# TensorE's queue kept in the order of emission, with a new entry into each attention stage

## The chip, the cores and the metric

The kernel runs on one core of a Trainium2 chip. The metric is the device time of one execution in microseconds (us). Each engine of the core, TensorE (PE), VectorE (DVE), ScalarE (ACT), GpSimd (POOL) and SyncE (SP, which issues most DMAs), works through a queue of its own in order; an instruction whose input is not ready stands in its queue, and with it all that is behind it.

## The reference

Two identical layers act on a sequence of 256 tokens with 1024 features, in float32. One layer is:

```
h    = rmsnorm(x) ; proj = h @ w_in                      # 1024 x 7704
out_a = dilated_mixer(rope(rmsnorm(qa)), rope(rmsnorm(ka)), va)     # 24 heads of 64, 3 dilations
k_cmp, v_cmp = gelu(blocks of 32 tokens + pos @ cmp_w1) @ cmp_w2    # compressed keys and values
out_b = g0 * attention(qb, k_cmp, v_cmp) + g1 * attention(qb, k_sel, v_sel) + g2 * window(qb, k_win, v_win)
x = x + (sigmoid(m0) * (out_a @ w_proj_a) + sigmoid(m1) * (out_b @ w_proj_b)) @ w_out
h = rmsnorm(x) ; g, u = split(h @ w_up)                  # 1024 x 5632
x = x + (silu(causal_conv3(g)) * u) @ w_down             # 2816 x 1024
```

## The kernel before

**The weight stream.** All weights of a layer lie packed in units of 128 x 2048 floats, in the order of use. Each unit is loaded by SP in two halves into `raw` (five buffers, `load_half`), and `halve` in `prepare` splits each half into hi (ScalarE, L238) and lo (VectorE, L239), so that a float32 product is three fast matmuls: hi·hi, lo·hi and hi·lo (L290 to L292 with 512 columns of weights, L373 and L957 to L959 with 256 columns of tokens, L993 and L994 in the last projections). The splits lie in the list `pend`. `next_unit` hands out the next unit, loads the one after it, and casts at once what is due.

**The order of emission.** A layer's attention stage emits its weight chunks one after the other: c10 and c11 (compressed, selected and window keys and values, gates), bq (queries of mixer b), chunks 0 to 8 (q, k and v of mixer a), four merge units for mixer b after the chunks 1, 2, 3 and 5 (`merge`), projection b, four merge units for mixer a, projection a, `out_proj`; then `ffn_up` and `ffn_down`. A chunk of 512 columns is two units, each used for both token tiles, 12 matmuls a tile. After every group of matmuls the code calls `tick`, which casts one half and advances each attention job by one step, and starts a waiting one if fewer than five are active:

```
    def tick(depth=5):
        if pend:
            pend.popleft()[1]()
        for g in list(chains):
            advance(chains, g)
        for g in list(active):
            advance(active, g)
```

A job is a Python generator that emits some instructions and gives way at each `yield`: `rope_run` (normalise and rotate a tile of q or k, then its `fin` transposes it), `job_cmp1` (lays the compressed mixer's tokens out), `job_cmp2` (hidden layer, gelu, compressed attention), `job_b` (one head pair and token tile of selected and window attention), `job_a` (the same for the dilated mixer). So the code's own order puts a job's small matmuls between the groups of 12 or 24 stream matmuls, and `yield` sets how many groups lie between a job's steps.

**The order of the queues.** The order of emission is not the order of the queues. The framework lists the instructions of every engine anew: with a cost model of its own it takes for each engine the instruction that it holds to be ready first, and among ready ones the one emitted first. Waits on other engines are semaphores put in afterwards. In TensorE's queue of this kernel a stream matmul can therefore stand ahead of a job's matmul that the code emits before it.

**The entry of an attention stage.** In layer 0 the `start` pool holds the input (`xo`, with tokens in the order of residues), which SP loads between the first weight halves. `feed` scales it by the norm's gain into hi and lo parts of `hT`, squares it and sums the squares over the eight feature tiles: for tiles 0 to 3 of the first input the squares are GpSimd's, and the sums are GpSimd's too, but for the last (`fin`, VectorE, L333). `rstd_col` (L344) sums over partitions by two matmuls and takes the root on GpSimd; `dg` (L351, VectorE) is a diagonal matrix with the result, and `rstd_row` spreads it along the tokens by a matmul. Meanwhile GpSimd makes the rope tables `tabs` and `tabc` from `gr`, SP's load at L387. In layer 1 and ahead of the feed-forward, `feed` is called as the tiles of x are finished. In `rope_b`, `fin` copies the rotated keys into `rd` (L482) and at once transposes them (L485); `job_cmp1` copies into `cdup` (L792) and at once transposes (L795), then ScalarE copies the result into T2 in eight copies.

**job_cmp2.** L841 transposes the hidden layer, ScalarE copies it (L845), VectorE and a tanh (L851) make the gelu and `hr` (L855), L864 multiplies by cmp_w2, a chain of normalisation and rope ends with a copy (L876), L879 transposes, L891 scores, a softmax ends at `es` (L910), L914 transposes that. Between the steps stand one or two `yield`. It starts when the last w1 unit is through, and is emitted in the same ticks as `job_a`, whose eight exponentials are at L664.

Of the kernel before, what the change touches and what calls it, by code (L numbers as in the profile page):

```python
# [11 lines left out]
F32 = mybir.dt.float32  # L12
# [7 lines left out]
P = 128  # L20
D = 1024
S = 256
# [142 lines left out]
def block_kernel(ctx, tc, x_in, xo_in, ws, g_norm, g_rope, pos, w2, conv, rope_c, ropec_c, mask_c, misc_c, out):  # L165
# [17 lines left out]
    G.memset(warm, 0.0)  # L183
    A.activation(warm, warm, AF.Square)
    gain = com.tile([P, 2 * DEPTH, 8], F32, name="gain")
    ones = com.tile([P, P], F32, name="ones")
    G.memset(ones, 1.0)
    ident = com.tile([P, P], F32, name="ident")
    make_identity(nc, ident)
    masks = com.tile([P, 1152], F32, name="masks")  # L190
    misc = com.tile([P, 96], F32, name="misc")
# [23 lines left out]
    def prepare(upto):  # L215
        while nxt[0] < len(units) and nxt[0] <= upto:
            i = nxt[0]
            u = units[i][1:]
            ffn = u[0] in ("up", "down")
            if ffn and ffn_pool[0] is None:  # L220
                return
            if u[0] == "w1":
                split[i] = [load_half(i, c0, UW // 2) for c0 in (0, UW // 2)]
                nxt[0] += 1
                continue
            w = _unit_width(u)
            pool, nb = (ffn_pool[0], 1) if ffn and ffn_turn(i) else (com, 2)
            hi = pool.tile([P, UW], F32R, name="hi", bufs=nb)
            lo = pool.tile([P, UW], F32R, name="lo", bufs=nb)
            for c0 in (0, w // 2):  # L230
                if (i, c0) in early:
                    raw = early.pop((i, c0))
                else:
                    raw = load_half(i, c0, w // 2)
                c = slice(c0, c0 + w // 2)
# [69 lines left out]
    def feed(u, m, gi, permute, src=None):  # L305
# [6 lines left out]
        else:  # L312
            for t in range(2):
                tok = slice(t * P, (t + 1) * P)
                v = by_residue(src[:, m:m + 1, tok], t)[:, 0]
                hi, lo = [u[:, i, m, tok].rearrange("p (r i) -> p r i", r=4) for i in range(2)]
                A.activation(hi, v, AF.Copy, scale=gc)
                V.scalar_tensor_tensor(lo, v, gc, hi.bitcast(F32), op0=ALU.mult, op1=ALU.subtract)
        if m == 0:
            sums["acc"] = com.tile([P, S], F32, name="acc2", bufs=1)  # L320
        sq = sums["acc"] if m == 0 else com.tile([P, S], F32, name="sq", bufs=2)
        if src is not x and m < 4:
            G.tensor_tensor(sq, xm, xm, op=ALU.mult)
        else:
            A.activation(sq, xm, AF.Square)
        if m == 0:
# [14 lines left out]
    def rstd_col():  # L341
# [8 lines left out]
        for t in range(2):  # L350
            V.tensor_scalar(dg[:, t * P:(t + 1) * P], ident, r[:, 1, t:t + 1], None, op0=ALU.mult)  # L351
        sums["dg"] = dg
# [22 lines left out]
    def attention_layer(l, pool, hT):  # L375
# [16 lines left out]
        nc.sync.dma_start(w2t, w2[l].rearrange("p (a b d) -> p a b d", a=2, b=2))  # L392
        for a in range(2):
            G.tensor_tensor(tabs[:, a], cossin[:, a, :, None, :].to_broadcast([P, 2, 5, 64]),
                            gr[:, a, None, 0:5, :].to_broadcast([P, 2, 5, 64]), op=ALU.mult)
        tabc = pool.tile([P, 2, 64], F32, name="tabc")
        G.tensor_tensor(tabc, ropec, gr[:, :, 5, :], op=ALU.mult)
# [4 lines left out]
        qS = pool.tile([P, 2, 4, S], F32R, name="qS")  # L402
        bigF = pool.tile([P, 2, 16, 2, 16], F32, name="F", tag="bigF", bufs=1)
# [17 lines left out]

        def rope_run(raw, kind, t, nh, ksc, fin):
            t1 = pool.tile([P, 8, 64], F32, name="t1", bufs=4)[:, :nh]
# [9 lines left out]
            if ksc is None:  # L433
# [5 lines left out]
                            op=ALU.mult)  # L439
            V.tensor_add(t1, t1, t2)  # L440
            yield
            yield
            fin(t1)

        def chunk_in(c, ncols, post_fn):
            ps = [acc(), acc()]
            for kh in range(2):
                hi, lo = next_unit(1 if c == "c10" and kh == 1 else 2)
                hi = hi[:, :4 * ncols].rearrange("p (k n) -> p k n", k=4)
                lo = lo[:, :4 * ncols].rearrange("p (k n) -> p k n", k=4)  # L450
                for t in range(2):
                    for k in range(4):
                        kk = kh * 4 + k
                        tok = slice(t * P, (t + 1) * P)
                        mm3(ps[t][:, :ncols], hT[:, 0, kk, tok], hT[:, 1, kk, tok], hi[:, k], lo[:, k],
                            kh == 0 and k == 0, kh == 1 and k == 3)
                    if kh == 1:
                        if c == "c10" and t == 0:
                            nrm["col"] = rstd_col()
                        post_fn(t, ps[t])  # L460
# [17 lines left out]

        def rope_b(b, t):
            def fin(r):  # L480
                rd = pool.tile([P, 2, 2, 64], F32, name="rd", tag="t2", bufs=1)
                V.tensor_copy(rd, r[:, 0:2, None, :].to_broadcast([P, 2, 2, 64]))  # L482
                ps = att()
# [5 lines left out]
                ready["b"] += 1  # L489
            start(rope_run(kraw[:, t, b].rearrange("p (h d) -> p h d", d=64), 3 + b, t, 2, None, fin))  # L490

# [295 lines left out]
        def job_cmp1():  # L787
            for kv in range(2):
                ps = att()
                dup = pool.tile([P, 2, 2, 2, 64], F32, name="cdup", tag="pT", bufs=5)  # L790
                for h in range(2):
                    V.tensor_copy(dup[:, h], craw[:, :, 2 * kv + h, None, :].to_broadcast([P, 2, 2, 64]))  # L792
                for h in range(2):
                    for t in range(2):
                        T.transpose(ps[:, (2 * h + t) * P:(2 * h + t + 1) * P],  # L795
                                    dup[:, h, t].rearrange("p a d -> p (a d)"), ident)
                T2 = pool.tile([P, 2, 264], F32, name="T2", tag="pt", bufs=4)
                for t in range(2):
                    src = ps.rearrange("p (h t r i) -> p h t r i", h=2, t=2, r=4)[:, :, t]
                    for u in range(2):  # L800
                        c0 = t * P + 1 - u
                        A.copy(by_residue(T2[64 * u:64 * u + 64, :, c0:c0 + P], t), src[64 * u:64 * u + 64])
                if kv == 0:
# [32 lines left out]
        def job_cmp2():  # L836
# [85 lines left out]
            for i in range(2):  # L922
# [98 lines left out]
    def ffn_up(l, pool, u, act):  # L1021
# [135 lines left out]
```

## Time and profile before

| | |
|---|---|
| median of three runs | 968.22 us (965.47 to 968.27) |
| the profiled execution | 964.59 us |
| its span, first to last instruction | 962.8 us |
| granted TensorE clock, mean | 1.00 |
| busy: PE, DVE, ACT, POOL | 936.6, 753.0, 580.2, 154.7 us |
| DMA | 165.95 MB, 172 GB/s on average |

The times of single instructions come from the profiled execution, whose own time is 1.8 us longer than its span. The clock column is the share of full speed that the throttle granted. A matmul's recorded duration covers its way through the pipeline; successive ones overlap, so the distance between their starts is what each costs.

### The profile page before, as it was taken

To read this page: it belongs to the slowest core of one execution; us is meant where nothing else is said; L and a number is where in the kernel's file an instruction comes from. 1 tells how busy PE (TensorE), PEld (TensorE's weight loads), DVE (VectorE), ACT (ScalarE), POOL (GpSimd) and SP (SyncE) were. 2 spreads that over 40 slices of the span, in tenths; PEclk is the share of its full clock that TensorE was granted. 3 is DMA by queue.
4 is the path that set the end of the run, shared out by engine and by line. 5 is a ranking of instruction groups with operands and counts; after the bars stand their busy time and mean duration, and the time that the engine had idled before them with its cause. 6 is when DMAs were issued, how large, how long until landed. Compare 5 with 4: busy or idle time off the path is not lost.

```text
span 962.8 us, 18575 instructions
## 1 busy us (share of the span) xinstructions
PE 936.6 (97%) x7122; PEld 848.9 (88%) x7122; DVE 753.0 (78%) x1595; ACT 580.2 (60%) x1186; POOL 154.7 (16%) x179
## 2 busy tenths in 40 slices
PE   6899999999999999999998999999999999999998
PEld 4778887878999999999986787877799999999998
DVE  6898866887679889986478987678876888998742
ACT  6778665666556555555456986466755555655431
POOL 6140211212002111110122301122200111111000
PEclk9999999999999999999999999999999999999999
DMA  7734446525456565666455344554354465666660
GB/s 242 255 132 155 150 157 207 189 88 174 148 162 213 180 210 187 189 196 204 147 168 174 112 151 135 196 196 140 121 180 153 161 217 175 205 197 203 196 209 19
DMA packets 48041, 165.95 MB, mean 172 GB/s; under 512 B 6096, under 2 KB 7632, under 8 KB 47824
## 3 DMA queue, kind: packets, MB, share of 16 engines
q1 hardware_dynamic: 46800, 163.71, 52.1%
q8 instruction: 56, 0.92, 0.4%
q10 hardware_dynamic: 1152, 1.05, 0.3%
q14 instruction: 33, 0.27, 0.1%
HBM read 163.69 MB, written 1.05 MB: 171 GB/s over the span
## 4 chain that ended last, share of the span: by engine, by line
PE 78%; DVE 10%; ACT 6%; issue 2%; POOL 1%; DMA 1%; SPq 0%; DVEq 0%; ACTq 0%; POOLq 0%
PE acc L373 25%; PE acc L290 5%; PE acc L292 5%; PE acc L291 5%; DVE lo L239 4%; PE acc L1082 4%; PE acc L1084 4%; PE acc L1083 4%; PE acc L957 3%; PE att L571 3%; PE acc L959 3%; PE acc L958 3%; PE att L576 2%; PE acc L993 2%; PE acc L994 2%
## 5 line engine op out<-in xcount | busy, mean ns | idle before, releaser
L239 DVE TENSOR_TENSOR lo<-raw,hi 128x1024 fp32r<-128x1024 f32 (+1 forms) x292 | 368.4, 1279 | 51.6 <-ACT hi L238 49.4
L238 ACT CAST hi<-raw 128x1024 fp32r<-128x1024 f32 (+1 forms) x292 | 294.0, 1037 | 150.9 <-PE acc L291 36.9
L373 PE MATMUL acc<-u,hi 128*128 128x256 f32 x1376 | 236.3, 277 | 0.0
L373 PEld LDWEIGHTS acc<-u,hi 128*128 128x128 f32 x1376 | 207.4, 188 | 0.1
L373 PE MATMUL acc<-u,lo 128*128 128x256 f32 x688 | 190.2, 276 | 0.0
L290 PE MATMUL acc<-hi,hT 128*128 128x512 f32 (+1 forms) x384 | 154.0, 401 | 8.7 <-ACT hi L238 8.7
L292 PE MATMUL acc<-lo,hT 128*128 128x512 f32 (+1 forms) x384 | 150.0, 391 | 5.2 <-DVE lo L239 5.1
L291 PE MATMUL acc<-hi,hT 128*128 128x512 f32 (+1 forms) x384 | 148.5, 387 | 0.0
L373 PEld LDWEIGHTS acc<-u,lo 128*128 128x128 f32 x688 | 129.1, 188 | 0.0
L1084 PE MATMUL acc<-act,lo 128*128 128x256 f32 x352 | 97.2, 276 | 0.0
L1082 PE MATMUL acc<-act,hi 128*128 128x256 f32 x352 | 97.2, 276 | 0.0
L1083 PE MATMUL acc<-act,hi 128*128 128x256 f32 x352 | 97.2, 276 | 0.0
L290 PEld LDWEIGHTS acc<-hi,hT 128*128 128x128 f32 x384 | 72.6, 189 | 25.9 <-ACT hi L238 11.1
L292 PEld LDWEIGHTS acc<-lo,hT 128*128 128x128 f32 x384 | 72.4, 189 | 23.6 <-DVE lo L239 9.2
L291 PEld LDWEIGHTS acc<-hi,hT 128*128 128x128 f32 x384 | 72.7, 189 | 12.6 <-issue 0.3
L957 PE MATMUL acc<-hT,hi 128*128 128x256 f32 x256 | 73.4, 287 | 0.0
L959 PE MATMUL acc<-hT,lo 128*128 128x256 f32 x256 | 71.8, 281 | 0.0
L958 PE MATMUL acc<-hT,hi 128*128 128x256 f32 x256 | 71.7, 280 | 0.0
L1084 PEld LDWEIGHTS acc<-act,lo 128*128 128x128 f32 x352 | 66.1, 188 | 0.0
L1082 PEld LDWEIGHTS acc<-act,hi 128*128 128x128 f32 x352 | 66.1, 188 | 0.0
L1083 PEld LDWEIGHTS acc<-act,hi 128*128 128x128 f32 x352 | 66.1, 188 | 0.0
L1054 POOL TENSOR_TENSOR z<-z,rb 128x512 f32<-128x512 f32 x22 | 30.5, 1386 | 203.1 <-DVE z L1053 203.1
(215 smaller groups left out, 1690.2 us busy)
## 6 DMA issues: line engine op xcount, KB each, us to landing
raw<-in_ws_dram SPq DMA_DIRECT2D x300, 512.0 KB, 4.6
raw<-in_ws_dram SPq DMA_DIRECT2D x8, 280.0 KB, 4.2
x<-in_x_dram SPq DMA_DIRECT2D x1, 1024.0 KB, 9.6
out_dram<-x ACTq DMA_DIRECT2D x8, 128.0 KB, 2.7
gr<-in_g_rope_dram SPq DMA_DIRECT2D x2, 384.0 KB, 4.4
masks<-in_mask_dram SPq DMA_DIRECT2D x1, 576.0 KB, 7.6
xo<-in_xo_dram SPq DMA_DIRECT2D x2, 256.0 KB, 4.5
xo<-in_xo_dram SPq DMA_DIRECT2D x1, 512.0 KB, 7.0
```

The lines of the kernel that those rows point to most:

```text
L238: A.copy(h, r)
L239: V.tensor_sub(l, r, h.bitcast(F32))
L290: T.matmul(o, a_hi, b_hi, start=first, stop=False)
L291: T.matmul(o, a_lo, b_hi, start=False, stop=False)
L292: T.matmul(o, a_hi, b_lo, start=False, stop=last)
L373: return [lambda a=a: T.matmul(a[0], a[1], a[2], start=a[3], stop=a[4]) for a in todo]
L957: T.matmul(o, hi[:, k, ms], hT[:, 0, k], start=k == 0, stop=False)
L958: T.matmul(o, hi[:, k, ms], hT[:, 1, k], start=False, stop=False)
L959: T.matmul(o, lo[:, k, ms], hT[:, 0, k], start=False, stop=k == 7)
L1082: T.matmul(ps, hi[:, c], act[:, 0, k], start=k == 0, stop=False)
L1083: T.matmul(ps, hi[:, c], act[:, 1, k], start=False, stop=False)
L1084: T.matmul(ps, lo[:, c], act[:, 0, k], start=False, stop=k == NFT - 1)
```

## The change

Seven things are changed.

1. TensorE's instructions keep the order in which the code emits them (`manual_schedule` for PE). The other engines' queues are ordered as before.
2. The start: 14 idle matmuls on `ones`; the input's first loads and `gain` are issued from ScalarE's queue and the table load for Square stands behind them; SP's first four loads are quarters of a unit, and the first unit is cast in quarters, each ahead of the `feed` of one tile.
3. The input's squares are ScalarE's, two tiles at a time, and their sums VectorE's. `dg` goes to ScalarE.
4. `qS` is allocated ahead of the tables, so that it and not `gr` comes to lie where `xo` was. The tables are made in three steps, the later ones by a side job.
5. c10 goes through its first unit by k instead of by token tile, and calls rstd_col and both `post_c10` at its end; c11 goes by token tile.
6. `rd` is copied two ticks ahead of its transposes, `cdup` one tick; `job_cmp1` starts behind c11 instead of ahead of it, transposes with a permutation, and copies T2 in two copies a head pair instead of four. `job_b` waits one more tick.
7. Ahead of the feed-forward, rstd_col goes from place 42 of the first unit's 48 matmuls to place 3 of the second unit's; the row sum and the first gate move by three places.

```diff
@@ block_kernel
-    A.activation(warm, warm, AF.Square)
+    idle = att()
+    for i in range(14):
+        T.matmul(idle[:, 0:P], ones, ones, start=True, stop=True)
@@ prepare
-            for c0 in (0, w // 2):
+            step = w // 4 if (i, w // 4) in early else w // 2
+            for c0 in range(0, w, step):
@@ feed
+        if src is not x:
+            if m % 2:
+                sq = com.tile([P, 2, S], F32, name="sq2", bufs=2)
+                A.activation(sq, src[:, m - 1:m + 1], AF.Square)
+                if m > 1:
+                    V.tensor_add(sq, sq, sums["acc"])
+                sums["acc"] = sq
+            if m == 7:
+                sums["fin"] = com.tile([P, S], F32, name="fin", bufs=1)
+                V.tensor_add(sums["fin"], sq[:, 0], sq[:, 1])
+            return
...
-        if src is not x and m < 4:
-            G.tensor_tensor(sq, xm, xm, op=ALU.mult)
-        else:
-            A.activation(sq, xm, AF.Square)
+        A.activation(sq, xm, AF.Square)
@@ rstd_col
-            V.tensor_scalar(dg[:, t * P:(t + 1) * P], ident, r[:, 1, t:t + 1], None, op0=ALU.mult)
+            A.activation(dg[:, t * P:(t + 1) * P], ident, AF.Copy, scale=r[:, 1, t:t + 1])
@@ attention_layer
+            for t in range(2):
+                V.tensor_copy(by_residue(perm[:, t:t + 1], t)[:, 0], ident.rearrange("p (r i) -> p r i", r=4))
...
+        qS = pool.tile([P, 2, 4, S], F32R, name="qS")
         tabs = pool.tile([P, 2, 2, 5, 64], F32, name="tabs")
...
+        table(3, 5)
@@ rope_run
             V.tensor_add(t1, t1, t2)
+            if pre:
+                pre(t1)
             yield
             yield
             fin(t1)
@@ chunk_in
+            if c == "c11":
+                unit(0)
+                for t in range(2):
+                    for kh in range(2):
+                        if t == 0 and kh == 1:
+                            unit(1)
+                        mms(kh, t, range(4), kh == 0, kh == 1)
+                        if kh == 1:
+                            post_fn(t, ps[t])
+                        tick()
+                return
...
+                if c == "c10" and kh == 0:
+                    for k in range(4):
+                        for t in range(2):
+                            mms(0, t, [k], k == 0, False)
+                        if k % 2:
+                            tick()
+                    continue
@@ rope_b
+            def pre(r):
+                box["rd"] = pool.tile([P, 2, 2, 64], F32, name="rd", bufs=2)
+                V.tensor_copy(box["rd"], r[:, 0:2, None, :].to_broadcast([P, 2, 2, 64]))
@@ job_b
             while ready["b"] < 6:
                 yield
+            yield
@@ job_cmp1
-                ps = att()
                 dup = pool.tile([P, 2, 2, 2, 64], F32, name="cdup", tag="pT", bufs=5)
                 for h in range(2):
                     V.tensor_copy(dup[:, h], craw[:, :, 2 * kv + h, None, :].to_broadcast([P, 2, 2, 64]))
+                yield
+                ps = att()
...
-                                    dup[:, h, t].rearrange("p a d -> p (a d)"), ident)
+                                    dup[:, h, t].rearrange("p a d -> p (a d)"), perm[:, t])
...
+                for u in range(2):
+                    r = slice(64 * u, 64 * u + 64)
+                    A.copy(T2[r, :, 1 - u:1 - u + S], ps[r].rearrange("p (h q) -> p h q", h=2))
@@ attention_layer, its sequence
+        def job_tables():
+            table(2, 3)
+            yield
+            table(0, 2)
+            yield
+            G.tensor_tensor(tabc, ropec, gr[:, :, 5, :], op=ALU.mult)
...
         chunk_in("c10", 512, post_c10)
+        side.append(job_tables())
+        chunk_in("c11", 280, post_c11)
         side.append(job_cmp1())
-        chunk_in("c11", 280, post_c11)
@@ ffn_up
-                pg = unit({42: rstd_col}, True)
-                pu = unit({24: lambda: box.update(rb=rstd_row()), 30: lambda: post_g(0, pg)})
+                pg = unit({}, True)
+                pu = unit({3: rstd_col, 27: lambda: box.update(rb=rstd_row()), 33: lambda: post_g(0, pg)})
@@ block_kernel, its start
-        nc.sync.dma_start(xo[:, 0:2], xv[:, 0:2])
-        nc.sync.dma_start(gain, g_norm.rearrange("p (a k) -> p a k", k=8))
-        early[0, 0] = load_half(0, 0, UW // 2)
+        A.dma_start(xo[:, 0:2], xv[:, 0:2])
+        A.dma_start(gain, g_norm.rearrange("p (a k) -> p a k", k=8))
+        A.dma_start(xo[:, 2:4], xv[:, 2:4])
+        A.activation(warm, warm, AF.Square)
+        quarters(0, 0)
...
-        nc.sync.dma_start(xo[:, 2:4], xv[:, 2:4])
-        early[0, UW // 2] = load_half(0, UW // 2, UW // 2)
+        quarters(0, 1)
         nc.sync.dma_start(xo[:, 4:8], xv[:, 4:8])
...
+        prepare(0)
         for m in range(8):
-            if m in (1, 3):
-                if m == 1:
-                    prepare(0)
+            feed(hT, m, 0, False, xo)
+            if m < 4:
                 pend.popleft()[1]()
-            feed(hT, m, 0, False, xo)
@@ kernel
     with tile.TileContext(nc) as tc:
-        block_kernel(tc, *args)
+        with tc.manual_schedule(engines={mybir.EngineType.PE}):
+            block_kernel(tc, *args)
```

`quarters(i, h)` loads half h of unit i into one `raw` buffer by two DMAs of 512 columns each; `table(k0, k1)` makes the tables k0 to k1 - 1 with two multiplications on GpSimd.

## Rows read from the trace of the kernel before

**Rows 1.** The page's first part: busy time, share and instructions of each engine.

```profile
PE 936.6 (97%) x7122; PEld 848.9 (88%) x7122; DVE 753.0 (78%) x1595; ACT 580.2 (60%) x1186; POOL 154.7 (16%) x179
```

**Rows 2.** Busy time by stretch: PE, PEld, DVE, ACT, POOL, clock, DMA, GB/s.

```profile
40.00:60.00 20.00, 19.22 (x92) 15.25 (x91) 19.60 (x35) 12.87 (x21) 4.62 (x2) 1.00 0.63 210
...
340.00:360.00 20.00, 20.00 (x179) 20.00 (x178) 18.69 (x23) 10.78 (x16) 2.62 (x2) 1.00 0.62 199
```

**Rows 3.** TensorE's waits by releaser: total us, times, longest us.

```profile
PE acc L290 <- ACT hi L238: 8.7, 4, 7.1
PE acc L292 <- DVE lo L239: 5.1, 8, 2.2
PE att L344 <- DVE fin L333: 3.1, 2, 1.6
PE att L485 <- DVE rd L482: 2.6, 2, 1.8
PE att L795 <- DVE cdup L792: 1.9, 2, 1.5
```

**Rows 4.** Instructions in order of time, layer 0's entry: start, duration, engine, line.

```profile
7.08 0.80 PE L290 MATMUL acc<-hi,hT 128*128 128x512 f32 x1 [7.08 <-ACT hi L238]
...
11.98 0.40 PE L290 MATMUL acc<-hi,hT 128*128 128x512 f32 x1
...
13.37 0.39 PE L290 MATMUL acc<-hi,hT 128*128 128x512 f32 x1
...
15.39 0.33 SPq L387 DMA_DIRECT2D gr<-in_g_rope_dram  x1
...
21.46 2.10 DVE L351 TENSOR_SCALAR dg<-ident,rstd 128x128 f32<-128x128 f32 x2
```

**Rows 5.** The same view of VectorE, layer 1's entry.

```profile
494.99 0.48 DVE L351 TENSOR_SCALAR dg<-ident,rstd 128x128 f32<-128x128 f32 x2
```

**Rows 6.** The same view around job_cmp2, layer 0, and one row of layer 1.

```profile
167.25 0.38 PE L841 MATMUL att<-ident,hid 128*128 128x128 f32 x2
...
168.93 0.44 ACT L664 ACTIVATE pt<-pt,nb 128x128 f32<-128x128 f32 x1
...
172.68 0.36 ACT L845 COPY gl<-att 128x256 f32<-128x256 f32 x1
...
172.98 0.28 PE L957 MATMUL acc<-hT,hi 128*128 128x256 f32 x1
...
176.78 0.29 DVE L853 SCALAR_TENSOR_TENSOR gl<-gl 128x128 f32<-128x128 f32 x1
...
178.13 0.41 DVE L855 TENSOR_SCALAR hr<-gl 128x512 f32<-128x512 f32 x1
...
178.63 1.08 PE L864 MATMUL att<-w2t,hr 128*128 128x64 f32 x8
...
653.26 1.05 PE L864 MATMUL att<-w2t,hr 128*128 128x64 f32 x8
```

**Rows 7.** The same view, the rest of job_cmp2 in layer 0.

```profile
184.13 0.18 DVE L876 COPY cs<-cs 128x64 f32<-128x64 f32 x1
...
188.39 1.06 PE L891 MATMUL att<-kf,qS 128*128 128x32 f32 x8
...
197.32 0.42 DVE L910 TENSOR_TENSOR es<-es,sm 128x256 f32<-128x256 f32 x1
```

**Rows 8.** The same view of VectorE, the end of layer 0's attention.

```profile
270.56 0.42 DVE L296 TENSOR_TENSOR oTa<-res,oTa 128x256 fp32r<-128x256 f32 x1
...
284.63 0.68 DVE L296 TENSOR_TENSOR hT<-tha,hT 128x512 fp32r<-128x512 f32 x1
```

**Rows 9.** The same view of VectorE, layer 0's bq chunk.

```profile
55.01 0.29 DVE L482 COPY rd<-t 128x256 f32<-128x256 f32 x1
```

**Rows 10.** The same view, first and last of six short sites.

```profile
93.19 0.37 ACT L579 COPY pT<-att 128x256 f32<-128x256 f32 x1 [0.55 <-PE att L576]
...
259.13 2.35 DVE L239 TENSOR_TENSOR lo<-raw,hi 128x1024 fp32r<-128x1024 f32 x2
```

More of the change, by code (lines that the diff above doesn't have):

```diff
@@ L188, in block_kernel @@
     ident = com.tile([P, P], F32, name="ident")
+    idle = att()
+    for i in range(14):
+        T.matmul(idle[:, 0:P], ones, ones, start=True, stop=True)
     make_identity(nc, ident)
+    perm = com.tile([P, 2, P], F32, name="perm")
     masks = com.tile([P, 1152], F32, name="masks")
@@ L233, in prepare @@
                 else:
-                    raw = load_half(i, c0, w // 2)
-                c = slice(c0, c0 + w // 2)
+                    raw = load_half(i, c0, step)
+                c = slice(c0, c0 + step)
                 def halve(h=hi[:, c], l=lo[:, c], r=raw):
@@ L392, in attention_layer, with table @@
         nc.sync.dma_start(w2t, w2[l].rearrange("p (a b d) -> p a b d", a=2, b=2))
-        for a in range(2):
-            G.tensor_tensor(tabs[:, a], cossin[:, a, :, None, :].to_broadcast([P, 2, 5, 64]),
-                            gr[:, a, None, 0:5, :].to_broadcast([P, 2, 5, 64]), op=ALU.mult)
+        def table(k0, k1):
+            for a in range(2):
+                G.tensor_tensor(tabs[:, a, :, k0:k1], cossin[:, a, :, None, :].to_broadcast([P, 2, k1 - k0, 64]),
+                                gr[:, a, None, k0:k1, :].to_broadcast([P, 2, k1 - k0, 64]), op=ALU.mult)
+        table(3, 5)
         tabc = pool.tile([P, 2, 64], F32, name="tabc")
-        G.tensor_tensor(tabc, ropec, gr[:, :, 5, :], op=ALU.mult)
         qscA = pool.tile([P, 2, 4, 3, 2], F32, name="qscA")
@@ L401, in attention_layer @@
         qscB = pool.tile([P, 2, 8], F32, name="qscB")
-        qS = pool.tile([P, 2, 4, S], F32R, name="qS")
         bigF = pool.tile([P, 2, 16, 2, 16], F32, name="F", tag="bigF", bufs=1)
@@ L420, in attention_layer, with rope_run @@
         ready = {"b": 0, "o": 0, "t": 0, 0: 0, 1: 0, 2: 0, 3: 0}
-        def rope_run(raw, kind, t, nh, ksc, fin):
+        def rope_run(raw, kind, t, nh, ksc, fin, pre=None):
             t1 = pool.tile([P, 8, 64], F32, name="t1", bufs=4)[:, :nh]
@@ L446, in chunk_in, with unit, mms @@
             ps = [acc(), acc()]
-            for kh in range(2):
-                hi, lo = next_unit(1 if c == "c10" and kh == 1 else 2)
-                hi = hi[:, :4 * ncols].rearrange("p (k n) -> p k n", k=4)
-                lo = lo[:, :4 * ncols].rearrange("p (k n) -> p k n", k=4)
-                for t in range(2):
[L452 to L458, printed above, removed]
+            un = {}
+            def unit(kh):
+                un[kh] = [z[:, :4 * ncols].rearrange("p (k n) -> p k n", k=4)
+                          for z in next_unit(1 if c == "c10" and kh == 1 else 2)]
+            def mms(kh, t, ks, first, last):
+                for k in ks:
+                    tok = slice(t * P, (t + 1) * P)
+                    mm3(ps[t][:, :ncols], hT[:, 0, kh * 4 + k, tok], hT[:, 1, kh * 4 + k, tok], un[kh][0][:, k],
+                        un[kh][1][:, k], first and k == ks[0], last and k == ks[-1])
+            if c == "c11":
[9 more added lines that the diff above has]
+                return
+            for kh in range(2):
+                unit(kh)
+                if c == "c10" and kh == 0:
[5 more added lines that the diff above has]
+                    continue
+                for t in range(2):
+                    mms(kh, t, range(4), kh == 0, kh == 1)
+                    if kh == 1 and (c != "c10" or t == 1):
+                        if c == "c10":
                             nrm["col"] = rstd_col()
+                            post_fn(0, ps[0])
                         post_fn(t, ps[t])
@@ L479, in rope_b @@
         def rope_b(b, t):
+            box = {}
+            def pre(r):
+                box["rd"] = pool.tile([P, 2, 2, 64], F32, name="rd", bufs=2)
+                V.tensor_copy(box["rd"], r[:, 0:2, None, :].to_broadcast([P, 2, 2, 64]))
             def fin(r):
-                rd = pool.tile([P, 2, 2, 64], F32, name="rd", tag="t2", bufs=1)
-                V.tensor_copy(rd, r[:, 0:2, None, :].to_broadcast([P, 2, 2, 64]))
+                rd = box["rd"]
                 ps = att()
@@ L489, in fin @@
                 ready["b"] += 1
-            start(rope_run(kraw[:, t, b].rearrange("p (h d) -> p h d", d=64), 3 + b, t, 2, None, fin))
+            start(rope_run(kraw[:, t, b].rearrange("p (h d) -> p h d", d=64), 3 + b, t, 2, None, fin, pre))
         def post_bq(t, ps):
@@ L795, in job_cmp1 @@
                         T.transpose(ps[:, (2 * h + t) * P:(2 * h + t + 1) * P],
-                                    dup[:, h, t].rearrange("p a d -> p (a d)"), ident)
+                                    dup[:, h, t].rearrange("p a d -> p (a d)"), perm[:, t])
                 T2 = pool.tile([P, 2, 264], F32, name="T2", tag="pt", bufs=4)
[L798 to L802, printed above, removed]
+                for u in range(2):
+                    r = slice(64 * u, 64 * u + 64)
+                    A.copy(T2[r, :, 1 - u:1 - u + S], ps[r].rearrange("p (h q) -> p h q", h=2))
                 if kv == 0:
@@ L1095, in block_kernel, with quarters @@
         xv = xo_in.rearrange("p (k q) -> p k q", k=8)
-        nc.sync.dma_start(xo[:, 0:2], xv[:, 0:2])
-        nc.sync.dma_start(gain, g_norm.rearrange("p (a k) -> p a k", k=8))
-        early[0, 0] = load_half(0, 0, UW // 2)
+        def quarters(i, h):
+            raw = com.tile([P, UW // 2], F32, name="raw", bufs=5)
+            for j in range(2):
+                c = slice(j * 512, (j + 1) * 512)
+                early[i, h * 1024 + j * 512] = raw[:, c]
+                nc.sync.dma_start(raw[:, c], ws[i][:, h * 1024 + j * 512:h * 1024 + (j + 1) * 512])
+        A.dma_start(xo[:, 0:2], xv[:, 0:2])
[3 more added lines that the diff above has]
+        quarters(0, 0)
         mhalf = com.tile([P, 16], F32, name="mhalf")
         G.memset(mhalf, -0.5)
-        nc.sync.dma_start(xo[:, 2:4], xv[:, 2:4])
-        early[0, UW // 2] = load_half(0, UW // 2, UW // 2)
+        quarters(0, 1)
         nc.sync.dma_start(xo[:, 4:8], xv[:, 4:8])
```

## The prediction, made before the changed kernel was run

> **What bounds the kernel now.** I read the page first, then the busy time by stretch, then TensorE's waits, then the order of time around each of them. TensorE (PE) is busy 97% of the span [rows 1], and its granted clock is 1.00 in every stretch [rows 2]. In the feed-forward stretches it issues 179 matmuls of 256 columns in 20 us without a hole [rows 2], 0.112 us each; a 512-column one takes (13.37 - 11.98)/6 = 0.232 us [rows 4]. From 40 to 60 us VectorE (DVE) is as full as TensorE, 19.60 of 20 us [rows 2]. So a microsecond that TensorE stands still is a microsecond of the span, nearly everywhere, and the question is only which standstills go and which come. The waits of before are few [rows 3]: 8.7 us for hi (7.1 of it the start, so 1.6 us later), 5.1 us for lo, 3.1 us for fin, 2.6 us for rd and 1.9 us for cdup; 14.3 us over both layers after the first matmul. The reader should also see that the queue of before is not the order in which the code emits: L957 at 172.98 and the 23 merge matmuls behind it stand ahead of L864 at 178.63 [rows 6], though the loop emits L864 first.
>
> **Part 1: the entry.** All of it removes waits; I price it by the waits themselves.
>
> *First matmuls.* From 7.08 up to 11.98 us TensorE issued nine 512-column matmuls in 4.9 us; at 0.232 us they take 2.1 [rows 4]. The first took 0.80 us where those after 11.98 took 0.40: they ran at the lower of the two clock levels, though the clock column shows 1.00, and in front of them the engine had done nothing. The 14 idle matmuls stand there now, in time that was empty; two instructions each, at half speed some 0.22 us (twice the 0.112), 28 x 0.22 = 6.2 us from about 1 us, so at worst they end as late as the first real one began. Gain 2.8 us; bounds 1.0 (the weights' arrival sets the pace instead) and 3.8 (the first matmul also starts 1.0 us earlier). The quarter loads and ScalarE's three issues serve this term and get no price of their own: the first weight half stood behind xo and gain on SP's queue and is now first there. What hides the added table load and issues on ScalarE is the wait for xo.
>
> *cdup and rd.* job_cmp1 now emits its copies one tick before the transposes, and rd is copied two ticks before its transposes. Both waits go: 1.9 + 2.6 = 4.5 us [rows 3]; bounds 3.0 and 4.5.
>
> *hi and lo.* 6.7 us in all [rows 3]. Less work stands before them: T copies go from eight of 256 columns to four of 512 per layer, dg goes from VectorE to ScalarE, which is busy 60% of the span [rows 1], squares go from GpSimd to ScalarE, sums to VectorE while it waits for data, qS takes xo's place in memory so that SP's load of gr no longer stands until 15.39 us in front of the weights [rows 4]. Against it: VectorE is full from 40 us on [rows 2]. I take half less a little, 3.0 us; bounds 1.0 and 5.0. dg took 2.10 us in layer 0, beside GpSimd's tables, and 0.48 us in layer 1 [rows 4, 5]. The Trainium skill (SBUF — State Buffer, Summary: rules for kernel authors) says that of VectorE with two SBUF inputs and GpSimd the second to issue blocks until the first is done, and dg's 2.10 against 0.48 agrees with it; by that rule all 6.7 us would go, and the sum below would be 9.6 instead of 13.3.
>
> *fin.* Two waits, 3.1 us [rows 3]. rstd_col moves from place 42 of 48 to place 3 of the next unit, nine matmuls later: 9 x 0.112 = 1.0 us each. Gain 2.0; bounds 1.0 and 3.0. The row sum still has 24 matmuls (2.7 us) of cover for its chain through GpSimd.
>
> Entry together: 2.8 + 4.5 + 3.0 + 2.0 = **12.3 us gained**, bounds 6.0 and 16.3.
>
> **Part 2: the order.** Nothing is added to the work. But where the queue of before let later matmuls pass one whose input was late, TensorE now stands. For each such place I take the moment at which the code's order reaches the instruction, and the moment at which its input was written in the trace; queued behind it is everything TensorE has, and behind that the casts and evacuations. Times are of layer 0; layer 1 repeats them, 474.6 us later (L864 at 653.26) [rows 6].
>
> *L864 (job_cmp2).* After L841 at 167.25 the loops emit 12 chunk matmuls and 24 of merge's first half, which end as L957 starts at 172.98. hr (L855) is written at 178.13 + 0.41 = 178.54 [rows 6]: 5.6 us. It is late because ScalarE copies the hidden layer (L845, 172.68) only behind eight exponentials of a job_a in the same tick, which run from 168.93, and because VectorE puts lo conversions between. Neither job is edited. I take 5.0, since one lo conversion may fall out. Lower bound 2.2: from L845's end at 173.04 five VectorE steps of about 0.29 as L853's, a tanh of about 0.36 as L845's, and hr's 0.41 [rows 6].
>
> *L879.* After L864 (1.08 us) the code emits 24 merge matmuls and ten transposes, which I price alike: 178.63 + 1.08 + 34 x 0.112 = 183.5. cs is written at 184.31 [rows 7]: 0.8; bounds 0 and 1.0 (a chain without company, or L864 taking no more than the 0.9 until its successor).
>
> *L914.* After L891, which ends at 189.45, come 24 chunk matmuls (24 x 0.232 = 5.6 us) and six transposes (0.7), so 195.7; es is written at 197.74 [rows 7]: 2.0; bounds 0.5 and 2.7.
>
> *The last job_a, projection a, out_proj.* oTa's lo is written at 270.98, hT's last lo at 285.31 [rows 8]. In order the projection reaches its k = 3 some 0.9 us early after a wait of 0.4 for pT; out_proj's first tile reaches the last rows of hT about 1.6 early, where before its second tile went ahead. 2.7; bounds 2.0 and 2.9.
>
> *bq.* rd at 55.01 [rows 9] (written at 55.30) would cost 2.5 us at its turn, 52.8; the earlier copy takes that away, and job_b's added yield puts 12 matmuls (2.8 us) before the first scores. But VectorE is full here, so the softmaxes stay late: 1.0; bounds 0 and 2.5.
>
> *Six short ones* of 0.1 to 0.5 us, the first for a pT copy (L579, written at 93.56), the last for a lo conversion (L239, written at 260.36) that the queue of before went around [rows 10]: 1.3; bounds 0.6 and 1.3.
>
> Together 5.0 + 0.8 + 2.0 + 2.7 + 1.0 + 1.3 = 12.8 a layer, **25.6 us lost** in two, bounds 10.6 and 32.
>
> **Sum.** 25.6 - 12.3 = 13.3 us slower. The profiled execution took 964.6 us (span 962.8 and 1.8 around it), so 977.9; the runs shown have their median at 968.2, 3.6 above it, so 981.5 us.
>
> **The rivals.**
>
> *The waits dissolve (faster).* All rests on one place: L845 behind L664 on ScalarE. If the new order puts the copy ahead, hr's chain (0.36 + 0.36 + 5 x 0.29 + 0.41 = 2.6 us) starts at 167.6 and ends by 170.3, before 172.98 [rows 6]; and once TensorE stands, hi and lo conversions find no free buffer and leave VectorE to the short chains at L879 and L914. Then the 2.7 of the layer's end and 0.9 of the short ones stay, 3.6 a layer: 7.2 - 12.3 = -5.1, 963 us. It decides once L864 waits under 1.5 us. For it: ScalarE is 60% busy. Against it: the exponentials are emitted first and were ready first. 0.16.
>
> *Half.* L864 falls to its lower bound, 2.2, and the other 7.8 by half: 6.1 a layer, 12.2 against 12.3, 968 us. For it: of the 5.1 us between L845's end and hr's start only 5 x 0.29 + 0.36 = 1.8 are the chain's own [rows 6]. 0.11.
>
> *The entry is won and lost again.* VectorE, full from 40 us on, sets the end of that stretch however early the entry is done: the gain is 6.0 us, the waits stay 25.6: +19.6, 988 us. For it rows 2; against it that dg and the contention leave VectorE. 0.11.
>
> **How the numbers follow.** The forecast (972 to 990 by itself: gains 9 to 14, losses 18 to 31) gets 0.62. The range 964 to 992 cuts half of the first rival at the low end and the outermost of the forecast and the third rival at the high end. About 0.3%, 2.9 us, is what a measurement of this kernel can tell from no change: faster 0.16 (the first rival), same 0.10 (the second), slower 0.74.
>
> **What would show it.** Right: TensorE's longest waits are L864 for hr, some 5 us twice, then L914, L994 or L373, L879; those for rd and cdup are gone, fin's are about 0.6 us each, the early 512-column matmuls take 0.40 us from the first, and layer 0's bq chunk starts some 5 us earlier than before. The order part is wrong if L864 waits under 1.5 us; the entry part is wrong if the gain at the end of bq in layer 0 is under 3 us. Either moves the sum past its range only together with the other.

## The result, and the profile after

The changed kernel takes 1000.32 us (median of five runs, 999.03 to 1003.92) against 967.44: 1.0347 times as long (95% interval 1.0326 to 1.0369), 32.9 us slower. The direction was forecast, the size was not: 13.3 us were expected, and 992 us was the top of the range. The profiled execution has a span of 997.2 us, 34.4 more than before, and took 999.03.

The first part of the page of the changed kernel (busy time and share of each engine), which answers to [rows 1]:

```profile
PE 950.4 (95%) x7150; PEld 865.0 (87%) x7150; DVE 748.2 (75%) x1594; ACT 579.4 (58%) x1188; POOL 144.4 (14%) x177
```

TensorE stands still for 997.2 - 950.4 = 46.8 us, 20.6 more than the 26.2 of before; that is what the forecast was about. But it is also busy for 13.8 us more, of which the 28 idle matmuls take 5.6. The rest, 8.2 us, lies in matmuls that take longer.

TensorE's waits in the changed kernel (total us, times, longest), which answer to [rows 3]:

```profile
PE att L913 <- DVE hr L904: 10.9, 2, 5.5
PE att L963 <- DVE es L959: 9.2, 2, 4.6
PE att L778 <- DVE mxb L785: 4.7, 4, 1.5
PE acc L296 <- DVE lo L243: 4.4, 6, 1.0
PE att L778 <- DVE qS L300: 2.1, 2, 1.3
PE att L644 <- DVE drb L809: 2.1, 2, 1.1
PE acc L294 <- ACT hi L242: 1.9, 1, 1.9
```

The lines have moved: L913 is L864 of before, L963 is L914, L778 is L728 (job_b's scores), L242 and L243 are the hi and lo conversions. The waits for rd, cdup and fin are gone. The longest two are where the forecast put them, for hr and for es.

Where the time goes can be read from when the same matmul starts in each trace. The table gives the start of the first matmul of a stage before (us), and by how much it is later in the changed kernel and in four experiments that are told below.

| first matmul of | before | changed | entry only | order only | filled | later |
|---|---|---|---|---|---|---|
| layer 0: c10 | 7.08 | +1.48 | +0.86 | +0.03 | +1.22 | +1.59 |
| bq | 32.70 | -2.21 | -1.65 | +3.70 | -2.42 | -1.74 |
| chunk 4 | 142.17 | +3.26 | -1.20 | +13.69 | +2.56 | +3.73 |
| projection b | 226.93 | +16.59 | -1.22 | +26.52 | +12.17 | +1.96 |
| feed-forward | 302.08 | +19.49 | -0.52 | +29.42 | +15.07 | +5.40 |
| down projection | 424.99 | +17.80 | -0.93 | +28.77 | +13.37 | +3.69 |
| layer 1: c10 | 484.83 | +17.80 | -0.93 | +28.77 | +13.37 | +3.69 |
| bq | 505.30 | +15.43 | -3.30 | +28.78 | +11.00 | +1.33 |
| chunk 4 | 615.80 | +20.82 | -2.92 | +37.91 | +16.90 | +5.29 |
| projection b | 701.52 | +33.32 | -2.63 | +52.94 | +26.77 | +4.22 |
| feed-forward | 776.65 | +36.25 | -1.93 | +55.85 | +29.44 | +6.92 |
| down projection | 899.56 | +34.56 | -2.88 | +55.21 | +27.74 | +5.22 |

In the changed kernel, up to bq 2.2 and 2.4 us are gained; from bq to chunk 4 5.5 and 5.4 are lost; from chunk 4 to projection b, where job_cmp2 runs, 13.3 and 12.5; from there to the feed-forward 2.9 and 2.9, and 1.7 of these come back at its entry.

The stretch of the first long wait in the changed kernel, busy time of TensorE, granted clock, DMA share and GB/s:

```profile
176.00:179.00 3.00, 0.41 (x4) 1.00 0.00 0
179.00:182.00 3.00, 0.14 (x1) 0.62 0.28 45
182.00:185.00 3.00, 3.00 (x14) 0.50 0.75 279
185.00:188.00 3.00, 3.00 (x22) 0.74 0.06 26
188.00:191.00 3.00, 3.00 (x20) 1.00 0.00 0
```

And its matmuls (start, duration):

```profile
176.13 0.28 PE L1016 MATMUL acc<-hT,lo 128*128 128x256 f32 x1
181.86 1.97 PE L913 MATMUL att<-w2t,hr 128*128 128x64 f32 x8 [5.45 <-DVE hr L904]
183.59 0.56 PE L1014 MATMUL acc<-hT,hi 128*128 128x256 f32 x1
183.95 0.41 PE L1015 MATMUL acc<-hT,hi 128*128 128x256 f32 x1
184.16 0.41 PE L1016 MATMUL acc<-hT,lo 128*128 128x256 f32 x1
...
186.66 0.28 PE L1016 MATMUL acc<-hT,lo 128*128 128x256 f32 x1
186.78 0.28 PE L1014 MATMUL acc<-hT,hi 128*128 128x256 f32 x1
```

TensorE waits 5.45 us for hr; in the wait the clock falls to 0.50, the lower of its two levels (1.2 instead of 2.4 GHz), and stays there after the wait has ended. L913's eight matmuls take 1.97 us (1.08 before [rows 6]), and those behind it stand 0.21 us apart instead of 0.12, until 186.5. The mean clock of before was 1.00, of the changed kernel 0.986, and the forecast had no term for it.

### The profile page after: what moved, and what is told of

The parts are those of the page before. It is cut to its first block, busy times and chain, and to the rows that moved or that the text cites. A ratio compares the mean times of both kernels' runs of the same rounds, so it can differ in the third digit from the quotient of the medians.

```text
span 997.2 us, 18622 instructions
## 1 busy us (share of the span) xinstructions
PE 950.4 (95%) x7150; PEld 865.0 (87%) x7150; DVE 748.2 (75%) x1594; ACT 579.4 (58%) x1188; POOL 144.4 (14%) x177
## 3 DMA queue, kind: packets, MB, share of 16 engines
q10 hardware_dynamic: 1584, 1.59, 0.5%
## 4 chain that ended last, share of the span: by engine, by line
PE 79%; DVE 12%; ACT 5%; issue 2%; POOL 1%; DMA 1%; SPq 0%; ACTq 0%; DVEq 0%
PE acc L385 28%; PE acc L294 6%; PE acc L296 5%; PE acc L295 5%; DVE lo L243 4%; PE acc L1140 4%; PE acc L1141 4%; PE acc L1139 4%; PE acc L1014 3%; PE acc L1016 3%; PE acc L1015 3%; PE att L620 2%; PE att L625 2%; ACT pt L713 2%; PE acc L1051 1%
## 5 line engine op out<-in xcount | busy, mean ns | idle before, releaser
L243 DVE TENSOR_TENSOR lo<-raw,hi 128x1024 fp32r<-128x1024 f32 (+2 forms) x294 | 368.1, 1269 | 57.6 <-ACT hi L242 56.2
L242 ACT CAST hi<-raw 128x1024 fp32r<-128x1024 f32 (+2 forms) x294 | 294.1, 1030 | 155.9 <-PE acc L295 55.8
L295 PE MATMUL acc<-hi,hT 128*128 128x512 f32 (+1 forms) x384 | 149.5, 389 | 0.0
L294 PEld LDWEIGHTS acc<-hi,hT 128*128 128x128 f32 x384 | 73.8, 192 | 19.6 <-issue 3.0
L295 PEld LDWEIGHTS acc<-hi,hT 128*128 128x128 f32 x384 | 73.7, 192 | 12.9
L1014 PE MATMUL acc<-hT,hi 128*128 128x256 f32 x256 | 74.7, 292 | 0.0
L1015 PE MATMUL acc<-hT,hi 128*128 128x256 f32 x256 | 72.8, 284 | 0.0
```

The source lines that it names most:

```text
L294: T.matmul(o, a_hi, b_hi, start=first, stop=False)
L295: T.matmul(o, a_lo, b_hi, start=False, stop=False)
L1014: T.matmul(o, hi[:, k, ms], hT[:, 0, k], start=k == 0, stop=False)
L1015: T.matmul(o, hi[:, k, ms], hT[:, 1, k], start=False, stop=False)
```

## The experiments

All times are medians; the kernel before ran beside each of them, at 966.5 to 967.8 us.

**Entry only and order only.** The two halves of the change, each by itself. Entry only is the changed kernel with

```diff
-        with tc.manual_schedule(engines={mybir.EngineType.PE}):
-            block_kernel(tc, *args)
+        block_kernel(tc, *args)
```

> The changed kernel without the fixed order of TensorE; the new entry stays. Theory A (the order alone is the loss, at its standstills and in the low clock behind them): between the first bq matmul and the end of out_proj the changed kernel lost 18.8 + 2.9 us in layer 0 and some 22 in layer 1, 43.9 in all; without it 1000.3 - 43.9 = 956. Rival B (the order costs the 25.6 us of the forecast, and the entry loses the rest instead of gaining): 1000.3 - 25.6 = 975, slower than before.

and order only is the kernel before with the opposite edit.

> The kernel before with nothing but the fixed order of TensorE. Theory A: 967.4 + 43.9 = 1011 us, and up to 5 more, since rd and cdup are copied late here and TensorE's queue can no longer go round them. Rival B: 967.4 + 25.6 = 993 us.

Measured: 961.89 us for the entry alone (ratio 0.9947, interval 0.9928 to 0.9965) and 1017.71 for the order alone (1.0522, 1.0499 to 1.0545). Rival B falls: the entry is no loss, and the order costs twice the forecast. Theory A is nearer, but both runs came out above it (by 6 us and by 2 to 7): the two parts don't simply add up. The order costs 51.2 us on the old entry and 1000.3 - 961.9 = 38.4 on the new one; the entry brings 4.6 us under the old queue and 17.4 under the fixed one.

**Standstill filled.** Is it the standstill that makes the clock fall? The changed kernel with matmuls that compute nothing in the time in which TensorE stood, in front of L913 and of L963 (there 17 of them, into `p2`):

```diff
             ps = att()
+            for i in range(21):
+                T.matmul(ps[:, 256:384], ones, ones, start=True, stop=True)
             for kv in range(2):
```

> The changed kernel with 21 matmuls on ones in front of L913 and 17 in front of L963, in the time in which TensorE stands there (42 x 0.112 = 4.7 of 5.45 us, 34 x 0.112 = 3.8 of 4.58). Theory clock (the standstill makes TensorE's clock fall, and what follows is slow): the 2.3 us lost in and behind L913 and the 1.9 behind L963 come back in both layers, 1000.3 - 8.4 = 992 us, with granted clock 1.00 there. Rival (the slow matmuls behind the waits have another cause, or the wait is just as long and costs only itself): 1000.3 us, no change.

Measured: 993.53 us, 6.8 less, with more work in the program. The same stretch in this run, and its matmuls:

```profile
176.00:179.00 3.00, 3.00 (x30) 1.00 0.00 0
179.00:182.00 3.00, 2.23 (x21) 1.00 0.46 135
182.00:185.00 3.00, 3.00 (x28) 1.00 0.68 213
```

```profile
175.54 4.85 PE L912 MATMUL att<-ones 128*128 128x128 f32 x42
181.16 1.10 PE L915 MATMUL att<-w2t,hr 128*128 128x64 f32 x8 [0.77 <-DVE hr L904]
182.07 0.36 PE L1018 MATMUL acc<-hT,hi 128*128 128x256 f32 x1
182.27 0.28 PE L1019 MATMUL acc<-hT,hi 128*128 128x256 f32 x1
182.39 0.28 PE L1020 MATMUL acc<-hT,lo 128*128 128x256 f32 x1
```

hr comes as late as in the changed kernel (0.77 + 4.85 is the wait), but the clock stays at 1.00, L913's matmuls take 1.10 us and the next stand 0.12 apart: 28 instructions between 182 and 185 us instead of 14. From chunk 4 to projection b the loss falls from 13.3 and 12.5 us (table) to 9.6 and 9.9, about what the two waits amount to (5.4 + 4.6). So the clock's share behind these four waits is shown: 6.8 us of the 32.9. The Trainium skill (TensorE: Matmul & The Clock Gate, Why this matters for your kernels) has the rule that spoke for this: idle gaps between bursts of matmuls put the engine back to the low rate. This trace agrees, at 0.50 behind the wait of 5.45 us.

**Later steps of job_cmp2.** The changed kernel with two yields more ahead of L913 and two ahead of L963:

```diff
                             0.5, None, op0=ALU.mult)
             yield
+            yield
+            yield
             give("pT", 2)
```

> The changed kernel with two more yields in front of L913 and two in front of L963, so that TensorE has 2 x 12 or 24 more stream matmuls (5.5 us) ahead of each. Theory A (hr and es are late by a fixed chain, and the order of emission comes to them too early): the two waits, 10.0 us a layer, and the low clock behind them, 4.2, go: 1000.3 - 28.4 = 972 us. Rival (the chain on VectorE stands behind the casts that the same ticks bring, so it moves with the yields): the waits stay over 3 us each, 990 to 1000 us.

Measured: 969.13 us (1.0032, 1.0016 to 1.0047), 31.2 less. Theory A holds, and more than its sum comes back. The longest waits left:

```profile
PE att L778 <- DVE mxb L785: 4.6, 4, 1.5
PE acc L296 <- DVE lo L243: 2.8, 3, 1.0
PE att L625 <- DVE mxb L785: 2.2, 2, 1.1
```

Those for hr and es are gone, and from chunk 4 to projection b 1.8 and 1.1 us are gained. What is late here is not TensorE's order as such but the place of two steps in it: from the end of L841 to hr it takes 10.9 us in every trace that was read (before, changed, entry only, order only, filled, later), whichever the order.

**job_b a tick later.** The run with later steps, and

```diff
             p0 = softmax(0, s0)
+            yield
             s1 = qk(1)
```

> The run with later job_cmp2 steps (969.1 us) and one more yield in job_b between the first softmax and the second scores. Theory buffers: the scores (L778) wait for mxb because all five attention banks of PSUM are still being read, and the fixed order puts the second scores in front of all else; a tick later a bank is free: the 4.6 us for mxb go and some of the 2.2 for qS and 2.2 for L625, 969.1 - 6 = 963 us. Rival (VectorE is full in this stretch, so the softmaxes are as late one tick later): within 1 us of 969.

Measured: 965.65 us, 3.5 less: between the two. What TensorE waits for in job_b's stretch now:

```profile
PE att L778 <- ACT qkT L602: 2.5, 2, 1.3
PE att L778 <- DVE qS L300: 2.1, 2, 1.3
PE att L625 <- DVE mxb L785: 2.0, 2, 1.0
```

The scores no longer wait for mxb but for ScalarE's copy of qkT (L602), which reads another attention bank of PSUM. Neither is an operand of the scores: both are readers of the bank that the scores overwrite. So the wait is for one of the five banks, as the theory has it; a tick later another reader is the one that holds it. The rival is not excluded, since qS and L625's mxb are as late as before: how the 5 us of this stretch divide between banks and a full VectorE stays open.

**Early copies alone.** The order-only kernel with rd copied two ticks and cdup one tick ahead, and job_b's added yield, as in the change:

```diff
             V.tensor_add(t1, t1, t2)
+            if pre:
+                pre(t1)
...
+                yield
+                ps = att()
```

> The kernel before with the fixed order (1017.7 us) and of the new entry only the early copies: rd two ticks ahead, cdup one, and job_b's added tick. Theory: in order these copies are what the entry is worth: the waits for rd (7.8) and cdup (1.9) go, with the low clock behind them (about 1.5 a layer) some 12 us, 1005 us. Rival: VectorE's and the start's relief are the larger part of the 17.4 us by which the entry helps in order, and the copies bring 4.5 as the forecast has it: 1013 us.

Measured: 1007.05 us, 10.7 less than order only. The theory holds: 10.7 of the 17.4 us that the entry is worth under the fixed order are these copies and job_b's tick; how they divide between the two wasn't tried.

**The start.** Entry only, with gain's load on SP's queue ahead of the weight quarters:

```diff
-        A.dma_start(gain, g_norm.rearrange("p (a k) -> p a k", k=8))
+        nc.sync.dma_start(gain, g_norm.rearrange("p (a k) -> p a k", k=8))
```

> The new entry without the fixed order (961.9 us), with the small load of gain issued from SP's queue ahead of the weight quarters. Theory: the late start of the changed kernel is gain's load, which landed 6.2 us after its issue beside the quarters, where it took 3.2 before; the first feed began at 7.49 us for it, before at 4.42. First feed at 4.5 to 5.5, first weight matmul 1.5 to 2.5 us earlier, 959 to 960.5 us. Rival: the quarters themselves or the tables' load set the start, and what is won there is waited for at the next lo: 961.9.

and the same without the 14 idle matmuls:

```diff
-    idle = att()
-    for i in range(14):
-        T.matmul(idle[:, 0:P], ones, ones, start=True, stop=True)
```

> The same as the run with gain first, without the 14 idle matmuls. Forecast's term: nine matmuls of 512 columns at the lower clock level cost 2.8 us, so 2 to 2.8 us slower than that run. Rival: the weights' arrival sets the pace of these matmuls anyway: under 1 us.

Measured: 962.54 and 962.07 us, against 961.89: no difference, and both rivals hold. The start of ScalarE and TensorE in the changed kernel:

```profile
7.49 0.51 ACT L314 ACTIVATE hT<-xo,gain 128x256 fp32r<-128x256 f32 x1 [3.83 <-DMA gain<-in_g_norm_dram]
7.91 0.60 ACT L242 CAST hi<-raw 128x512 fp32r<-128x512 f32 x1
```

```profile
1.05 5.57 PE L190 MATMUL att<-ones 128*128 128x128 f32 x28 [1.05 <-POOL ones L186]
8.56 0.51 PE L294 MATMUL acc<-hi,hT 128*128 128x512 f32 x1 [1.94 <-ACT hi L242]
...
10.31 0.63 PE L295 MATMUL acc<-hi,hT 128*128 128x512 f32 x1
10.73 0.63 PE L296 MATMUL acc<-lo,hT 128*128 128x512 f32 x1
```

with gain first:

```profile
4.87 0.51 ACT L314 ACTIVATE hT<-xo,gain 128x256 fp32r<-128x256 f32 x1 [1.69 <-DMA xo<-in_xo_dram]
7.10 0.62 ACT L242 CAST hi<-raw 128x512 fp32r<-128x512 f32 x1 [1.73 <-DMA raw<-in_ws_dram]
```

and without the idle matmuls:

```profile
7.93 0.79 PE L291 MATMUL acc<-hi,hT 128*128 128x512 f32 x1 [7.93 <-ACT hi L239]
8.52 0.63 PE L292 MATMUL acc<-hi,hT 128*128 128x512 f32 x1
...
11.21 0.40 PE L293 MATMUL acc<-lo,hT 128*128 128x512 f32 x1
```

In the changed kernel the first feed waits for gain until 7.49 us (before: 4.42), and behind the 1.94 us after the idle matmuls the clock is low again: from 9.88 to 12.44 us the weight matmuls stand 0.43 us apart. With gain first, the feed is 2.6 us earlier (2.0 earlier than in entry only, where it began at 6.88), and then the first weight quarter, issued at 1.18 us, is what comes at 7.10; the half of before, issued at 1.64, was there at 5.99. Four quarters under way side by side bring the first no sooner. The Trainium skill (DMA: Bandwidth & Descriptors, Issuing engines are not separate DMA queues) has it that SP's and ScalarE's loads go through the same DMA engines; the trace agrees, with gain landing 6.2 us after its issue beside the quarters and 3.2 before. Without idle matmuls the first six stand 0.43 us apart instead of 0.23, and yet c11 starts at 21.36 us instead of 21.20.

**Order in parts.** Three runs fix the order in some stretches only, by entering and leaving `manual_schedule` there. In the first, the kernel with job_b's yield leaves it from mixer a's merges to the feed-forward:

```diff
             if ab == "a":
+                order.__exit__(None, None, None)
```

> The run with job_b's added yield (965.7 us), with TensorE's order left to the framework from mixer a's merges to the end of out_proj, and fixed elsewhere. By the forecast's term for the layer's end (2.7 us a layer) and by the 2.9 that the changed kernel lost there: 965.7 - 5.6 = 960 us. Rival (what the queue of before won there depends on a disorder that begins earlier): 964 to 966 us.

Measured: 963.27 us, 2.4 less where 5.6 were expected, just below the rival's range. The loss from projection b to the feed-forward is gone but for 0.5 us in layer 1, and so is much of what followed it: from the feed-forward's start to the down projection the changed kernel makes up 1.7 us a layer, this run loses 0.2 in layer 0 and makes up 1.0 in layer 1. The tail's net loss in the changed kernel is therefore about 1.2 us a layer (16.59 to 17.80 in the table), not 2.9. That VectorE catches up while TensorE stands in out_proj is the likely reason: in order only, with the old entry, the waits for fin are 0.3 us in all instead of 3.1, and 0.6 us a layer come back there. It wasn't tried by itself.

In the second, entry only with the order fixed in c10, c11 and the feed-forward:

```diff
+        with tc.manual_schedule(engines={mybir.EngineType.PE}):
+            chunk_in("c10", 512, post_c10)
```

> The new entry without the fixed order (961.9 us), with the order fixed in c10, c11 and the feed-forward alone, where the changed kernel's milestones run ahead of that run's: about 1 us in layer 0's c10 and c11 and 0.8 at each feed-forward entry. If these gains are the order's: 959 to 960 us. Rival (they come from an earlier or later state of the neighbouring work): 961.5 to 962.5 us.

Measured: 963.44 us (961.34 to 964.67): no gain over entry only. The rival is nearer, and the run lies 1 us above its range too.

In the third, entry only with the order fixed from chunk 4 to chunk 8. The framework then also put bq and the chunks before in the order of emission, so the run holds more than was meant:

```diff
+            if c == 4:
+                order.__enter__()
             chunk_in(c, 512, post_a(c))
```

> The new entry (961.9 us), with the order fixed in the chunks 4 to 8 alone, where job_cmp2 runs. Theory (the standstills for hr, 5.4, and es, 4.6, and the low clock behind them, 3.7 a layer): 961.9 + 2 x 13 = 988 us. Forecast's terms (5.0 + 0.8 + 2.0 a layer, no clock): 961.9 + 15.6 = 977.5 us.

Measured: 998.52 us. As a sum it can't be held against either expectation, since bq's loss is in it. By stretches it can: from chunk 4 to projection b it loses 13.5 us in layer 0, as theory A has it (13), where the forecast's terms are 7.8; and all but 1.8 us of the whole loss is there without the order in the entry, the tail and the feed-forward.

## Why the prediction was wrong

**The step that failed first: "a microsecond that TensorE stands still is a microsecond of the span".** A standstill of several us costs more than itself, since the clock is low behind it. The rows for it were at hand: nine matmuls at half speed behind the idle start [rows 4], which the prediction read rightly, but only for the start, and didn't carry to the 5 us waits that it forecast itself. Shown by the filled run: 6.8 us.

The clock alone does not explain the miss: the filled run is still at 993.5 us, above the range's 992. Against the table the sum of 13.3 us falls 21.2 short: 10.2 from chunk 4 to projection b (of which the filled run, by the table, gives the clock 6.3), 6.3 from bq to chunk 4, 4.3 at the entry and 0.4 at the layer's end.

**L864 (5.0 us a layer)** was right: 5.45. The chain to hr is fixed, and TensorE's turn comes where it was worked out.

**L879 (0.8)** was nothing: at the low clock the 24 merge matmuls in front of it took 4.2 us (183.59 to 187.80) instead of 2.7, and cs was there. The clock is not the whole reason. In the filled run, at 1.00, there is no wait for cs either: it is written 3.6 us after the matmuls on hr end, where it took 4.6 before.

**L914 (2.0)** was mis-sized: 4.6. TensorE's turn was right, 6.3 us after the scores by the forecast (195.7 - 189.45) and 205.7 - 199.4 = 6.3 measured (L963's start at 210.29 less its wait of 4.58; the scores' end). But es was not carried over: its chain took 10.7 us from the end of the scores instead of 8.3. In the changed kernel VectorE's queue holds three lo conversions in it, the first already under way as the scores end; before, there was one:

```profile
196.18 1.22 DVE L239 TENSOR_TENSOR lo<-raw,hi 128x1024 fp32r<-128x1024 f32 x1
```

In the changed kernel:

```profile
199.10 1.22 DVE L243 TENSOR_TENSOR lo<-raw,hi 128x1024 fp32r<-128x1024 f32 x1
...
200.57 0.48 DVE L945 TENSOR_TENSOR es<-att,misc 128x128 f32<-128x128 f32 x2
...
201.80 1.22 DVE L243 TENSOR_TENSOR lo<-raw,hi 128x1024 fp32r<-128x1024 f32 x1
...
206.27 1.23 DVE L243 TENSOR_TENSOR lo<-raw,hi 128x1024 fp32r<-128x1024 f32 x1 [0.54 <-ACT hi L242]
...
209.72 0.43 DVE L959 TENSOR_TENSOR es<-es,sm 128x256 f32<-128x256 f32 x1
```

The last of them waits 0.54 us for its hi, whose cast at 205.19 had waited 0.59 us for TensorE's L295. It is the order that does this: the chain takes 10.7 us in order only too, and 8.3 and 8.6 in entry only. Holding TensorE's order re-sorted the queue of another engine, which the edit doesn't name; taking ready times from the trace of before was the error. That these conversions are the whole of the 2.4 us is read from the rows and wasn't tried by itself.

**bq and the six short ones (2.3)** were mis-sized: 5.5 and 5.4. rd is no longer late. The longest waits between bq and chunk 4 are those of job_b's scores for a bank that is still read (L778 for mxb, 2.3 us a layer), of which the forecast had no term, then those for qS (1.3 and 0.8) and drb (1.1 and 1.0), which VectorE writes late, and one of 1.1 at L625. In layer 1 the clock is low behind them as well, 0.57 from 555 to 559 us; in layer 0 it stays at 1.00. How the loss divides between banks and VectorE stays open, as said above.

**The layer's end (2.7)** was right where it was looked for, 2.9, but the order gives some of it back behind it: 0.6 us in order only.

**The entry (12.3, bounds 6.0 and 16.3)** brought 8.0 in the changed kernel by the table (2.2 + 2.4 up to bq, 2 x 1.7 at the feed-forward); of the 1.7, some 0.6 are the order's, by order only, and rd's part lies behind bq's first matmul. The first matmuls (2.8, lower bound 1.0) brought nothing: the weights set the pace, and "get no price of their own" missed that the quarters and the move to ScalarE's queue make the first feed 3 us late. The waits for cdup, rd and fin are gone, though fin's all but goes under the order alone. The waits for hi and lo fell by 2.3 us, not by the 3.0 taken nor wholly, as the sum of 9.6 had it: after the start, 4.4 us for lo are left of 6.7 for both. The prediction's own sign for a wrong entry part came true: at the end of bq in layer 0 the gain is 1.6 us (chunk 0 starts at 44.46 instead of 46.08), under 3. The order's sign did not, and the sum left its range all the same.

**The terms were added as if each stood alone.** The late copies of rd and cdup stand for 4.5 us of waits as long as the queue can go round them [rows 3]; when it can't, early copies, with job_b's tick, bring 10.7 us.

The table's own differences, in the prediction's terms, make up the whole: 10.9 (bq to chunk 4) + 25.8 (to projection b) + 5.8 (to the feed-forward) - 8.0 = 34.5 us, against a span that is 34.4 longer.

The best versions tried, entry only and its variants at 961.9 to 963.4 us, are some 0.4 to 0.55% faster than before, and don't differ clearly from each other.

## What to carry to other kernels

When an engine is held to the order of emission, price each place by the moment at which its input is ready, and then check whether the engines that make the input keep their own order; a list scheduler re-sorts them too. Add to a long standstill of TensorE the slow matmuls behind it: here 2.3 us behind 5.45 (0.9 in L913 and 14 x 0.1 after it). If the order is wanted, move the late steps back by the measured wait: four yields took 31 of 38 us out.

## What the runs showed of the hardware that was not expected

The low clock outlasts the standstill: behind the wait that ended at 181.86 it held until 186.5 us. Behind the idle matmuls ahead of the first real ones, the clock was 1.00 after 0.66 us of standing still (gain first) and low again after 1.94 us (changed kernel); two cases show no more than that. Without the fixed order the idle matmuls changed nothing, 962.54 us with them and 962.07 without. A 256 KB quarter load, issued at 1.18 us beside three others, was there at 7.10 us; a 512 KB half load, issued at 1.64 us behind loads of 256 and 16 KB, at 5.99.
